# Three orders of work in layer 0's attention of a two-layer decoder trunk

## The chip, the cores and the metric

The kernel runs on one core of one Trainium2 chip. The metric is the device time of one execution in microseconds (us), the median of several runs. A core has engines that each work through their own list of instructions in order: PE (TensorE, matrix products), DVE (VectorE), ACT (ScalarE), POOL (GpSimd) and SP (SyncE, which issues most DMA transfers). An engine waits on semaphores that other engines or DMA queues raise. Matrix products go into PSUM, from which DVE or ACT move them into SBUF.

## The reference

The trunk has two layers on one sequence of 1024 positions with a width of 1024, all in 32-bit floats; the inputs are activations, a memory of 256 rows, positions and the weights. Layer 0 mixes tokens with multi-head latent attention, where queries and keys are expanded from narrow projections and only a part of each head carries rotary positions; layer 1 uses a sliding window. Both add four heads that attend to the memory, and a squared-ReLU MLP follows each.

```python
MLA_HEADS, MLA_Q_RANK, MLA_KV_RANK = 12, 384, 256
MLA_NOPE, MLA_ROPE, MLA_V = 64, 32, 64

def mla_mixer(hn, positions, w_in, q_norm_g, kv_norm_g, w_uq, w_ukv):
    proj = hn @ w_in                       # c_q | c_kv | k_r | q_cross
    ...
    q = (rmsnorm(c_q, q_norm_g) @ w_uq).reshape(b, s, MLA_HEADS, MLA_QK)
    q = jnp.concatenate([q[..., :MLA_NOPE], rope(q[..., MLA_NOPE:], positions)], axis=-1)
    kv = (rmsnorm(c_kv, kv_norm_g) @ w_ukv).reshape(b, s, MLA_HEADS, MLA_NOPE + MLA_V)
    k_nope, v = kv[..., :MLA_NOPE], kv[..., MLA_NOPE:]
    k_rope = jnp.broadcast_to(rope(k_r[:, :, None, :], positions), (b, s, MLA_HEADS, MLA_ROPE))
    k = jnp.concatenate([k_nope, k_rope], axis=-1)
    o = causal_dense_attention(q, k, v)
    return o.reshape(b, s, MLA_HEADS * MLA_V), q_cross

def reference(x, mem, ...):
    mem_n = rmsnorm(mem, mem_norm_g)
    for i in range(DEPTH):                 # DEPTH = 2
        hn = rmsnorm(x, attn_norm_g[i])
        mix, q_cross = mla_mixer(...) if i % 2 == 0 else swa_mixer(...)
        cross = memory_cross_attention(q_cross, mem_n, w_mem_kv[i])
        x = x + jnp.concatenate([mix, cross], axis=-1) @ w_o[i]
        x = x + squared_relu_mlp(rmsnorm(x, mlp_norm_g[i]), mlp_w_up[i], mlp_w_down[i])
    return rmsnorm(x, final_norm_g)
```

## The kernel before, in words

Every large matrix product is made of three: each operand is split into a high part and a low part in a shorter format, and `mm3` or `mm3w` (lines 106 to 121) add high x high, high x low and low x high in PSUM. `split` (line 94) makes the two parts of a tile: ACT copies the high part (line 99, or 102 where a gain scales it), and DVE then subtracts it from the source (line 100, or 103). So whatever is split passes first ACT and then DVE.

The program is built by Python that traces the operations; a scheduler then gives every engine its list. It keeps the traced order unless something moves a block: `tc.issue_after(ins)` puts what is traced inside it behind the instruction `ins` on the engine of `ins`. It adds no wait, and the other engines' lists are ordered without it.

The change lies in the part of layer 0's attention that comes between the narrow projections and the scores (lines 785 to 985; in the profile about 174 to 250 us of 2090). It goes as follows.

*Keys.* A loop over `j`, six blocks of 128 rows of the keys' part without rotation (two heads each): 12 matmuls of 128x512 into `pskn{j}`, one of two PSUM buffers of 128x1024. DVE moves the first half of the columns out into `kn[j]` (shown as `kq`, line 934), ACT the second (line 935).

*Rope weights.* `load_cols` (line 703) is a generator that loads query weights in nine pieces: three blocks of rows `kt` by three thirds of the columns `i`, each a DMA of 192 KB on SP's queue into a staging tile `wraw` (shown as `wr`, with two buffers in turn, line 708), which is then split into high and low parts (`wqrh` on ACT, `wqrl` on DVE). A buffer is free for the next piece once DVE has made the low part. Each step of the generator makes one piece. At `j == 1` the kernel traces all nine pieces of the rotary columns at once.

*Queries.* For each of eight query tiles `t`, `q_rope` makes nine matmuls of 128x384 into `psqr{t}`, three for each block of rows `kt` of the weights, and DVE and POOL apply the rotation (lines 327 to 332). `q_ropeT` transposes the result of tile `t - 2` on PE (`psqt{t}`, line 962), and ACT moves it out (lines 963 and 964). The same loop loads the weights of the part without rotation (`wqn`) through `load_cols`. Then `q_nope(j, i)` makes that part into `psqn{j}_{i}`, moved out by ACT for `i` = 0 and by DVE for `i` = 1 (line 944).

*Head tiles.* `head_tiles(h)` gathers one head's 96 rows of queries and keys by four DMAs on SP's queue into `q32` and `k32` (one buffer each) and splits them. The split tiles of head 0 are `qh, ql, kh, kl`; those of head 1 reuse the memory of `ckh` and `ckl` and are shown by these names.

*Row maxima.* Between the `q_nope` steps, `row_max(0, i)` (line 896) makes the scores of eight row blocks of head 0 once (`psx`), and DVE takes the least negated value of each row into `m_0`. After the last, at `n == 8`, `max_row(0)` (line 884) transposes these values on PE (`psxt`), splits them (`mhl`), and two DMAs put them as a 97th row under the queries of head 0. At `n == 9` follows `head_tiles(1)`. The scores proper (`pss`, line 1038) come next.

`WoHalf` (line 785) loads and splits half of the output weights as a list of eight steps, `todo`; the main loop of the attention takes a step on every third turn from a fixed turn on.

Of the kernel before, what the change touches and what calls it, by code (L numbers as in the profile page):

```python
# [13 lines left out]
AF = mybir.ActivationFunctionType  # L14
# [41 lines left out]
def trunk(  # L56
# [7 lines left out]
    nc = tc.nc  # L64
# [4 lines left out]
    def pool(name, side="left", space=None, bufs=1):  # L69
        kw = {"reuse_waits": "tile"}  # L70
        if space is not None:
            kw["space"] = space
        return tc.alloc_tile_pool(name=name, bufs=bufs, side=side, **kw)
# [5 lines left out]
    def ps2(name):  # L79
        return psum[0].tile([P, 1024], F32, tag="s", bufs=2, name=name)  # L80

    def ps1(name):
        return psum[0].tile([P, 512], F32, tag="m", bufs=4 if len(psum) == 1 else 6, name=name)
# [9 lines left out]
    def f32(ap):  # L93
        return ap.bitcast(F32)

    def split(src, hi, lo, scale=None):

        if scale is None:
            a = nc.scalar.activation(hi, src, AF.Copy)  # L99
            d = nc.vector.tensor_tensor(lo, src, f32(hi), ALU.subtract)  # L100
        else:
            a = nc.scalar.activation(hi, src, AF.Copy, scale=scale)
            d = nc.vector.scalar_tensor_tensor(lo, src, scale, f32(hi), ALU.mult, ALU.subtract)
        return a.ins, d.ins
# [8 lines left out]
    def mm3w(pss, terms):  # L113

        n = len(terms)
        for i, (ah, al, bs) in enumerate(terms):
            for ps, (bh, bl) in zip(pss, bs):
                nc.tensor.matmul(ps, ah, bh, start=i == 0, stop=False)
                nc.tensor.matmul(ps, ah, bl, start=False, stop=False)
            for ps, (bh, bl) in zip(pss, bs):  # L120
                nc.tensor.matmul(ps, al, bh, start=False, stop=i == n - 1)
# [29 lines left out]
    g_q, g_kv, g_mem = gcol[:, 32:35], gcol[:, 35:37], gcol[:, 37:45]  # L151
# [186 lines left out]
    class MemProj:  # L338
# [3 lines left out]
        def __init__(self, layer, pl, src):  # L342
            self.layer, self.pl, self.src = layer, pl, src
# [356 lines left out]
    def wpair(pl, k, n, name, slot):  # L700
        return [pl.tile([P, k, n], F32R, tag=f"{slot}{e}", name=f"{name}{e}") for e in "hl"]

    def load_cols(src, nk, w, outs, g):

        for kt in range(nk):
            for i in range(3):
                raw = wu.tile([P, 4, w], F32, tag="wraw", bufs=2, name=f"wr{w}_{outs[0][1]}_{kt}_{i}")
                nc.sync.dma_start(out=raw.rearrange("p h c -> p (h c)"), in_=src[kt * P : (kt + 1) * P, i * 4 * w : (i + 1) * 4 * w])
                for dst, c0, n in outs:
                    o = [d[:, i * 4 * n : (i + 1) * 4 * n].rearrange("p (h c) -> p h c", c=n) for d in dst[kt]]  # L710
                    split(raw[:, :, c0 : c0 + n], *o, scale=g[:, kt : kt + 1])
                yield

    def rows(w, n):
        return [(w[0][:, k, :], w[1][:, k, :]) for k in range(n)]

    wkn, wkv = rows(wpair(wu, 2, 768, "wkn", "a"), 2), rows(wpair(wu, 2, 768, "wkv", "b"), 2)
    loading = load_cols(mla_w_ukv[0], 2, 128, [(wkv, 64, 64), (wkn, 0, 64)], g_kv)
# [66 lines left out]
    class WoHalf:  # L785


        def __init__(self, layer, half, slot):
            self.layer, self.half, self.slot = layer, half, slot
            self.raw, self.w = {}, []  # L790
            self.todo = [(self.load, 0), (self.load, 1), (self.split, 0), (self.load, 2), (self.split, 1), (self.load, 3), (self.split, 2), (self.split, 3)]

        def step(self):
            if self.todo:
                fn, j = self.todo.pop(0)
                fn(j)
# [61 lines left out]
    def head_ones(i):  # L858
        if i == 0:
            nc.gpsimd.memset(f32(bufs_[0][2][96:97]), 1.0)  # L860
            nc.gpsimd.memset(f32(bufs_[0][3][96:97]), 0.0)
        else:
            for e in (2, 3):
                nc.sync.dma_start(out=f32(bufs_[i][e][96:97]), in_=f32(bufs_[0][e][96:97]))


    def head_tiles(h):
        r = slice((h % 2) * 64, (h % 2) * 64 + 64)
        q32 = hb.tile([96, S], F32, tag="q32", bufs=1, name=f"q32_{h}")
        k32 = hb.tile([96, S], F32, tag="k32", bufs=1, name=f"k32_{h}")  # L870
        nc.sync.dma_start(out=q32[0:64], in_=qn[h // 2][r, :])
        nc.sync.dma_start(out=q32[64:96], in_=qr[h // 4][(h % 4) * 32 : (h % 4) * 32 + 32, :])
        nc.sync.dma_start(out=k32[0:64], in_=kn[h // 2][r, :])
        nc.sync.dma_start(out=k32[64:96], in_=krs)
        qh, ql, kh, kl = bufs_[h % 3]
        if h in (1, 2):
            head_ones(h)
        split(q32, qh[0:96], ql[0:96])
        split(k32, kh[0:96], kl[0:96])
# [3 lines left out]
    def max_row(h):  # L883
        qh, ql, kh, kl = bufs_[h % 3]
        pt = ps1(f"psxt{h}")[0:8, 0:P]
        nc.tensor.transpose(pt, m8s.pop(h), ident)
        if h:
            mh, ml = [at.tile([8, P], F32R, tag=f"m{e}", bufs=2, name=f"m{e}{h}") for e in "hl"]
        else:
            mhl = cp.tile([8, 2, P], F32R, tag="krT", bufs=1, name="mhl0")  # L890
            mh, ml = mhl[:, 0, :], mhl[:, 1, :]
        split(pt, mh, ml)
        nc.sync.dma_start(out=f32(qh[96:97, :]), in_=f32(mh))
        nc.sync.dma_start(out=f32(ql[96:97, :]), in_=f32(ml))

    def row_max(h, i):
        if h not in m8s:
            m8s[h] = hb.tile([P, NT], F32, tag="m8", bufs=2, name=f"m8_{h}")
        qh, ql, kh, kl = bufs_[h % 3]
        n = (i + 1) * P  # L900
        ps = psx(f"psx{h}_{i}") if i > 3 or len(psum) == 1 else ps1(f"psx{h}_{i}")
        cuts = [(0, 320), (320, 640)] if n == 640 else [(a, min(a + 512, n)) for a in range(0, n, 512)]
        if n == 640:
            ps = ps[:, 192:]
        for a, b in cuts:
            nc.tensor.matmul(ps[:, a:b], qh[0:96, i * P : (i + 1) * P], kh[0:96, a:b], start=True, stop=True, skip_group_check=True)  # L906
        m = m8s[h][:, i : i + 1]
        least = 3.0e38
        if h == 0 and i:
            nc.vector.reduce_max(m, ps[:, : n - P], axis=AX, negate=True)  # L910
            least = m
        o, k = (ps[:, n - P : n], dmask) if h == 0 else (ps[:, :n], wide[0][:, S - n :])
        nc.vector.tensor_tensor_reduce(o, o, k, -1.0, least, ALU.add, ALU.min, accum_out=m)  # L913
# [4 lines left out]
    kn = [kq[j // 4][:, j % 4, :] for j in range(6)]  # L918
# [5 lines left out]
    head_ones(0)  # L924
    nc.vector.tensor_copy(krs, krT)
    for j in range(6):
        if j == 1:
            wqr = rows(wpair(wu, 3, 384, "wqr", "b"), 3)
            for _ in load_cols(mla_w_uq[0], 3, 96, [(wqr, 64, 32)], g_q):
                pass  # L930
        ps = ps2(f"pskn{j}")
        mm3w([ps[:, s] for s in halves],
             [(wkn[kt][0][:, j * P : (j + 1) * P], wkn[kt][1][:, j * P : (j + 1) * P], [(ckh[:, kt, s], ckl[:, kt, s]) for s in halves]) for kt in range(2)])
        nc.vector.tensor_copy(kn[j][:, 0:512], ps[:, 0:512])
        nc.scalar.activation(kn[j][:, 512:1024], ps[:, 512:1024], AF.Copy)
    wu2 = pool("wu2", "right")
    wqn = rows(wpair(wu, 2, 768, "wqn", "a"), 2) + rows(wpair(wu2, 1, 768, "wqn2", "c"), 1)
    loading = load_cols(mla_w_uq[0], 3, 96, [(wqn, 0, 64)], g_q)

    def q_nope(j, i):  # L940
        ps = ps1(f"psqn{j}_{i}")
        mm3(ps, [(wqn[kt][0][:, j * P : (j + 1) * P], wqn[kt][1][:, j * P : (j + 1) * P], cTh[:, kt, halves[i]], cTl[:, kt, halves[i]]) for kt in range(3)])
        if i:
            nc.vector.tensor_copy(qn[j][:, halves[i]], ps)
        else:
            nc.scalar.activation(qn[j][:, halves[i]], ps, AF.Copy)
# [30 lines left out]
    for n in range(2, 12):  # L977
        q_nope(n // 2, n % 2)
        for i in range(2 * n - 4, min(2 * n - 2, NT)):
            row_max(0, i)  # L980
        if n == 8:
            max_row(0)
        if n == 9:
            head_tiles(1)
    wu2.release()
    wu.release()
    cp.release()
# [174 lines left out]
    for n in range(len(seq) + LB):  # L1162
# [17 lines left out]
        for g, i in ahead.get(n, ()):  # L1180
            if i < NT:
                row_max(g, i)
            else:
                max_row(g)
        h, j = divmod(n, NB)
# [1043 lines left out]
    for n, (c0, sink, j) in enumerate(jobs):  # L2229
# [17 lines left out]
        for i in range(2):  # L2247
            mid = crossing if n < 3 else swa if n > 5 else None
            ps = feat_mm(w, i, str(n + 2), mid and (lambda: next(mid, None)))
# [75 lines left out]
```

## Time and profile before

| what | value |
|---|---|
| median of 3 runs | 2091.8 us (2091.62 to 2091.94) |
| the profiled execution, own time | 2092.01 us |
| its span, first to last instruction | 2090.3 us |
| mean granted TensorE clock | 1.000 |
| PE busy | 2071.5 us, 99% of the span |
| DVE, ACT, POOL busy | 1474.9, 1109.8, 149.3 us (71%, 53%, 7%) |

The profile shows one execution. A row of a timeline gives the start and the length of an instruction in us, its engine, line, operation and tiles (written, then read after the arrow), how often it stands there in a row, and in brackets the idle time of its engine just before it, with what ended that time. A row of groups gives busy time and mean ns of one, then the idle time before. Matmuls overlap: the length of one is longer than the step from one to the next. SPq is the queue on which SP issues DMAs; the row of a DMA is its issue, not its transfer.

### The profile page before, as it was taken

To read this page: it belongs to the slowest core of one execution; us is meant where nothing else is said; L and a number is where in the kernel's file an instruction comes from. 1 tells how busy PE (TensorE), PEld (TensorE's weight loads), DVE (VectorE), ACT (ScalarE), POOL (GpSimd) and SP (SyncE) were. 2 spreads that over 40 slices of the span, in tenths; PEclk is the share of its full clock that TensorE was granted. 3 is DMA by queue.
4 is the path that set the end of the run, shared out by engine and by line. 5 is a ranking of instruction groups with operands and counts; after the bars stand their busy time and mean duration, and the time that the engine had idled before them with its cause. 6 is when DMAs were issued, how large, how long until landed. Compare 5 with 4: busy or idle time off the path is not lost.

```text
span 2090.3 us, 28907 instructions
## 1 busy us (share of the span) xinstructions
PE 2071.5 (99%) x9744; PEld 1690.3 (81%) x9744; DVE 1474.9 (71%) x2978; ACT 1109.8 (53%) x2396; POOL 149.3 (7%) x265
## 2 busy tenths in 40 slices
PE   9999999999999999999999999999999999999998
PEld 6988777778888888888888888778888888888887
DVE  8766778775977777976558534666977776976565
ACT  7554466666745544444445435766755444444453
POOL 1001001000000000000001133420000000000000
PEclk9999999999999999999999999999999999999999
DMA  6303233342444546944433544542344446944342
GB/s 225 104 1 84 51 70 92 102 146 87 140 153 151 167 152 233 330 132 157 136 116 110 148 100 124 142 132 84 126 153 165 161 142 233 327 145 156 118 120 91
DMA packets 182228, 292.86 MB, mean 140 GB/s; under 512 B 17739, under 2 KB 72128, under 8 KB 182080
## 3 DMA queue, kind: packets, MB, share of 16 engines
q1 hardware_dynamic: 175584, 272.60, 41.5%
q0 software_dynamic: 5168, 15.80, 2.1%
q10 hardware_dynamic: 1328, 2.63, 0.4%
q8 instruction: 76, 1.25, 0.2%
q14 instruction: 72, 0.59, 0.1%
HBM read 187.60 MB, written 81.44 MB: 129 GB/s over the span
## 4 chain that ended last, share of the span: by engine, by line
PE 94%; DVE 3%; ACT 1%; DMA 1%; issue 1%; POOL 0%; SPq 0%; DVEq 0%; ACTq 0%
PE psy L1897 6%; PE psy L1899 6%; PE psy L1898 6%; PE psu L1561 5%; PE psu L1560 5%; PE psu L1559 5%; PE psz L1898 4%; PE psz L1897 4%; PE psz L1899 4%; PE psv L1560 4%; PE psv L1561 4%; PE psv L1559 4%; PE pso L1068 3%; PE pss L1038 3%; PE pswo L109 3%; PE pswo L111 3%
## 5 line engine op out<-in xcount | busy, mean ns | idle before, releaser
L99 ACT ACTIVATE g<-i 128x512 fp32r<-128x512 f32 x79 | 49.9, 631 | 105.8 <-PE psy L1898 51.8
L1897 PE MATMUL psy<-g 128*128 128x512 f32 x256 | 100.0, 390 | 0.0
L1048 ACT ACTIVATE p<-pss 128x512 f32<-128x512 f32 (+2 forms) x144 | 68.8, 487 | 58.5 <-DVE pss L1046 50.1
L1898 PE MATMUL psy<-g 128*128 128x512 f32 x256 | 99.7, 389 | 0.0
L1899 PE MATMUL psy<-g 128*128 128x512 f32 x256 | 99.6, 389 | 0.0
L100 DVE TENSOR_TENSOR g<-i,g 128x512 fp32r<-128x512 f32 x79 | 55.3, 700 | 49.6 <-ACT g L99 49.6
L1068 PE MATMUL pso<-p,vf 128*128 128x512 f32 (+3 forms) x214 | 87.8, 492 | 0.0
L99 ACT ACTIVATE i<-mr 128x512 fp32r<-128x512 f32 x78 | 47.8, 627 | 72.3 <-PE psy L1898 23.6
L99 ACT ACTIVATE uh<-i 128x512 fp32r<-128x512 f32 x66 | 41.6, 631 | 82.9 <-PE psz L1898 38.4
L100 DVE TENSOR_TENSOR uh<-i,uh 128x512 fp32r<-128x512 f32 x66 | 45.6, 690 | 46.5 <-ACT uh L99 46.4
L913 DVE CUSTOM_DVE_ANT_0 psx<-psx,wide 128x1024 f32<-128x1024 f32 (+6 forms) x88 | 66.7, 760 | 14.8 <-PE psx L906 14.5
L1897 PE MATMUL psz<-g 128*128 128x512 f32 x192 | 74.7, 389 | 0.0
L1898 PE MATMUL psz<-g 128*128 128x512 f32 x192 | 74.7, 389 | 0.0
L1899 PE MATMUL psz<-g 128*128 128x512 f32 x192 | 74.7, 389 | 0.0
L1458 ACT ACTIVATE mr<-mr,gcol 128x256 f32<-128x256 f32 (+1 forms) x160 | 63.9, 475 | 13.2 <-DMA mr<-in_mlp_w_up_dram 11.8
L100 DVE TENSOR_TENSOR i<-mr,i 128x512 fp32r<-128x512 f32 x78 | 53.6, 687 | 23.7 <-ACT i L99 23.7
L1779 DVE TENSOR_TENSOR mqq<-mqf,mqq 128x512 f32<-128x512 f32 x64 | 43.1, 686 | 21.7 <-DMA mqf<-in_mlp_w_down_dram 21.6
L1899 PEld LDWEIGHTS psy<-g 128*128 128x128 f32 x256 | 48.1, 188 | 10.0
L1897 PEld LDWEIGHTS psy<-g 128*128 128x128 f32 x256 | 48.1, 188 | 9.8
L1898 PEld LDWEIGHTS psy<-g 128*128 128x128 f32 x256 | 48.1, 188 | 9.8
L1458 ACT ACTIVATE d<-d,gcol 128x256 f32<-128x256 f32 x128 | 53.6, 497 | 0.2 <-DMA d<-in_mlp_w_up_dram 0.2
L2154 ACT ACTIVATE sp<-sp,sst 128x257 f32<-128x257 f32 (+1 forms) x96 | 46.5, 488 | 13.0 <-DVE sst L2152 12.7
(674 smaller groups left out, 6847.9 us busy)
## 6 DMA issues: line engine op xcount, KB each, us to landing
i<-hd SPq DMA_DIRECT2D x154, 256.0 KB
hd<-uh SPq DMA_DIRECT2D x76, 256.0 KB
hd<-ul SPq DMA_DIRECT2D x76, 256.0 KB
mr<-in_mlp_w_up_dram SPq DMA_DIRECT2D x36, 512.0 KB
hd<-x SPq DMA_DIRECT2D x72, 256.0 KB
mr<-hd SPq DMA_DIRECT2D x70, 256.0 KB
d<-in_mlp_w_up_dram SPq DMA_DIRECT2D x32, 512.0 KB
mqf<-in_mlp_w_down_dram SPq DMA_DIRECT2D x32, 512.0 KB
```

What stands on the lines that cost most here:

```text
L99: a = nc.scalar.activation(hi, src, AF.Copy)
L100: d = nc.vector.tensor_tensor(lo, src, f32(hi), ALU.subtract)
L913: nc.vector.tensor_tensor_reduce(o, o, k, -1.0, least, ALU.add, ALU.min, accum_out=m)
L1048: masked[1:] = [nc.scalar.activation(p[:, c0:], ps, AF.Exp, scale=SC).ins]
L1068: mms.append(lambda: nc.tensor.matmul(o, a, b, skip_group_check=True, **kw))
L1458: nc.scalar.activation(w[:, k, :], w[:, k, :], AF.Copy, scale=g_mlp[layer][:, k0 + k : k0 + k + 1])
L1559: nc.tensor.matmul(ps, wh[:, k, :], xh[:, k, :], start=p in (1, 2, 5) and k == 0, stop=False, skip_group_check=True)
L1560: nc.tensor.matmul(ps, wh[:, k, :], xl[:, k, :], start=False, stop=False, skip_group_check=True)
L1561: nc.tensor.matmul(ps, wl[:, k, :], xh[:, k, :], start=False, stop=k == 3, skip_group_check=True)
L1897: nc.tensor.matmul(ps, ah[:, j, :], bh, start=start, stop=False, skip_group_check=True)
L1898: nc.tensor.matmul(ps, ah[:, j, :], bl, start=False, stop=False, skip_group_check=True)
L1899: nc.tensor.matmul(ps, al[:, j, :], bh, start=False, stop=k == NP - 1, skip_group_check=True)
```

## The change

There are three edits, and a step that does nothing.

1. The rope weights' pieces are no longer traced all together at `j == 1`. The generator is made at `j == 0`, and three pieces are traced after each of the first three blocks of keys, with their ACT parts behind that block's move on ACT.
2. `max_row` returns the two instructions of its split, and `head_tiles(1)` is traced behind both of them, on ACT and on DVE.
3. The list of steps of the output weights' half 0 of layer 0 gets a step without work before its last.

```diff
--- before.py
+++ after.py
@@ -789,6 +789,8 @@
             self.layer, self.half, self.slot = layer, half, slot
             self.raw, self.w = {}, []
             self.todo = [(self.load, 0), (self.load, 1), (self.split, 0), (self.load, 2), (self.split, 1), (self.load, 3), (self.split, 2), (self.split, 3)]
+            if layer == half == 0:
+                self.todo.insert(-1, (lambda j: None, 0))
 
         def step(self):
             if self.todo:
@@ -889,9 +891,10 @@
         else:
             mhl = cp.tile([8, 2, P], F32R, tag="krT", bufs=1, name="mhl0")
             mh, ml = mhl[:, 0, :], mhl[:, 1, :]
-        split(pt, mh, ml)
+        done = split(pt, mh, ml)
         nc.sync.dma_start(out=f32(qh[96:97, :]), in_=f32(mh))
         nc.sync.dma_start(out=f32(ql[96:97, :]), in_=f32(ml))
+        return done
 
     def row_max(h, i):
         if h not in m8s:
@@ -924,15 +927,16 @@
     head_ones(0)
     nc.vector.tensor_copy(krs, krT)
     for j in range(6):
-        if j == 1:
+        if j == 0:
             wqr = rows(wpair(wu, 3, 384, "wqr", "b"), 3)
-            for _ in load_cols(mla_w_uq[0], 3, 96, [(wqr, 64, 32)], g_q):
-                pass
+            loading = load_cols(mla_w_uq[0], 3, 96, [(wqr, 64, 32)], g_q)
         ps = ps2(f"pskn{j}")
         mm3w([ps[:, s] for s in halves],
              [(wkn[kt][0][:, j * P : (j + 1) * P], wkn[kt][1][:, j * P : (j + 1) * P], [(ckh[:, kt, s], ckl[:, kt, s]) for s in halves]) for kt in range(2)])
         nc.vector.tensor_copy(kn[j][:, 0:512], ps[:, 0:512])
-        nc.scalar.activation(kn[j][:, 512:1024], ps[:, 512:1024], AF.Copy)
+        with tc.issue_after(nc.scalar.activation(kn[j][:, 512:1024], ps[:, 512:1024], AF.Copy).ins):
+            for _ in range(3):
+                next(loading, None)
     wu2 = pool("wu2", "right")
     wqn = rows(wpair(wu, 2, 768, "wqn", "a"), 2) + rows(wpair(wu2, 1, 768, "wqn2", "c"), 1)
     loading = load_cols(mla_w_uq[0], 3, 96, [(wqn, 0, 64)], g_q)
@@ -979,9 +983,10 @@
         for i in range(2 * n - 4, min(2 * n - 2, NT)):
             row_max(0, i)
         if n == 8:
-            max_row(0)
+            done = max_row(0)
         if n == 9:
-            head_tiles(1)
+            with tc.issue_after(done[0]), tc.issue_after(done[1]):
+                head_tiles(1)
     wu2.release()
     wu.release()
     cp.release()
```

ScalarE (ACT) from the first block of keys on, before. `kq<-pskn` is a block's move out of PSUM, `wqrh<-wr_64_kt_i` the high part of the rope weights' piece (kt, i), and `kh<-k_0` the split of head 0's keys:

```order
L102 ACTIVATE wqrh<-wr_64_0_2_1981,gcol 128x128
L102 ACTIVATE wqrh<-wr_64_1_0_1985,gcol 128x128
L935 ACTIVATE kq_1942<-pskn_1956 128x512
L102 ACTIVATE wqrh<-wr_64_1_1_1989,gcol 128x128
L935 ACTIVATE kq_1942<-pskn_2009 128x512
L102 ACTIVATE wqrh<-wr_64_1_2_1993,gcol 128x128
L99 ACTIVATE kh_1951<-k_0_2342 96x1024
L102 ACTIVATE wqrh<-wr_64_2_0_1997,gcol 128x128
L935 ACTIVATE kq_1942<-pskn_2024 128x512
```

And now, from the move of block 0:

```order
L937 ACTIVATE kq_1942<-pskn_1958 128x512
L102 ACTIVATE wqrh<-wr_64_0_0_1973,gcol 128x128
L102 ACTIVATE wqrh<-wr_64_0_1_1977,gcol 128x128
L937 ACTIVATE kq_1942<-pskn_1985 128x512
L99 ACTIVATE kh_1951<-k_0_2342 96x1024
L102 ACTIVATE wqrh<-wr_64_0_2_1981,gcol 128x128
L102 ACTIVATE wqrh<-wr_64_1_0_2000,gcol 128x128
L937 ACTIVATE kq_1942<-pskn_2012 128x512
L102 ACTIVATE wqrh<-wr_64_1_1_2004,gcol 128x128
```

Four pieces stood ahead of block 0's move, and none does now; block 2's move, which had seven ahead of it, has four.

TensorE (PE) at the first rope matmuls of the queries, before (`psqr_2091`, `psqr_2117` and `psqr_2143` are query tiles 0, 1 and 2):

```order
L109 MATMUL psqr_2091<-wqrh,cTh 128x384
L110 MATMUL psqr_2091<-wqrl,cTh 128x384
L111 MATMUL psqr_2091<-wqrh,cTl 128x384
L109 MATMUL psqr_2117<-wqrh,cTh 128x384
L110 MATMUL psqr_2117<-wqrl,cTh 128x384
L111 MATMUL psqr_2117<-wqrh,cTl 128x384
```

And now, from the 18th of these matmuls to the first transpose (`psqt_2165` is that of tile 0):

```order
L111 MATMUL psqr_2143<-wqrh,cTl 128x384
L109 MATMUL psqr_2091<-wqrh,cTh 128x384
L109 MATMUL psqr_2117<-wqrh,cTh 128x384
L109 MATMUL psqr_2143<-wqrh,cTh 128x384
L110 MATMUL psqr_2091<-wqrl,cTh 128x384
L111 MATMUL psqr_2091<-wqrh,cTl 128x384
L110 MATMUL psqr_2117<-wqrl,cTh 128x384
L111 MATMUL psqr_2117<-wqrh,cTl 128x384
L110 MATMUL psqr_2143<-wqrl,cTh 128x384
L111 MATMUL psqr_2143<-wqrh,cTl 128x384
L966 MATMUL psqt_2165<-ident,fa_101 128x128 x3
```

Each tile's nine matmuls stood together; now tiles 0, 1 and 2 go through the first two row blocks of the weights first (18 matmuls), and then all three through the last.

VectorE (DVE) at the last row maximum of head 0 (`m_0`, `psx_7`), the split of the transposed maxima (`mhl`) and the splits of head 1 (`ckh`, `ckl`), before:

```order
L944 COPY qn_1941<-psqn_1_2442 128x512
L910 TENSOR_REDUCE m_0_2362<-psx_7_2426 128x1
L100 TENSOR_TENSOR ckh<-q_1_2482,ckh 96x1024
L913 ISA psx_7_2426,m_0_2362<-psx_7_2426,dmask,m_0_2362 128x128
L913 ISA m_0_2362 128x1
L100 TENSOR_TENSOR mhl_2466<-psxt_2464,mhl_2466 8x128
L944 COPY fa_101<-psqn_1_2471 128x512
```

And now:

```order
L913 TENSOR_REDUCE m_0_2362<-psx_7_2426 128x1
L916 ISA psx_7_2426,m_0_2362<-psx_7_2426,dmask,m_0_2362 128x128
L916 ISA m_0_2362 128x1
L100 TENSOR_TENSOR mhl_2466<-psxt_2464,mhl_2466 8x128
L100 TENSOR_TENSOR ckh<-q_1_2482,ckh 96x1024
L948 COPY fa_101<-psqn_1_2471 128x512
L100 TENSOR_TENSOR ckl<-k_1_2483,ckl 96x1024
```

The split of head 1's queries stood between the two steps of the last row block; it stands behind the split of the maxima now.

TensorE (PE) at the first score tile (`pss_1_0`), with the semaphores that it waits for, before and then now:

```order
L1038 MATMUL pss_1_0_2557<-qh_1949,kh_1951 128x512 [waits DMAHW0_49,Activation_49]
```

```order
L1043 MATMUL pss_1_0_2557<-qh_1949,kh_1951 128x512 [waits DMAHW5_49,DVE_49]
```

The matmul stands at the same place in the row, but its PSUM buffer is another: the engine that must have emptied it was ACT and is DVE.

## The prediction

> **What bounds the kernel now.** I read the page first: busy shares and the chain of waits.
>
> ```profile
> PE 2071.5 (99%) x9744; PEld 1690.3 (81%) x9744; DVE 1474.9 (71%) x2978; ACT 1109.8 (53%) x2396; POOL 149.3 (7%) x265
> PE 94%; DVE 3%; ACT 1%; DMA 1%; issue 1%; POOL 0%; SPq 0%; DVEq 0%; ACTq 0%
> ```
>
> TensorE sets the end. It has no slack in which a delay could vanish, and no engine after this stage gets another order, so a microsecond by which TensorE stands still longer or shorter here moves the end by a microsecond. The question is therefore only where PE waits between about 175 and 250 us, now and afterwards. The stretches by stage and the list of PE's waits answer the first half:
>
> ```profile
> 180.00:186.00 6.00, 5.24 (x24) 4.00 (x23) 2.63 (x5) 3.13 (x6) 0.00 (x0) 1.00 0.55 142
> 192.00:198.00 6.00, 6.00 (x38) 5.96 (x37) 6.00 (x17) 2.81 (x6) 2.80 (x5) 1.00 0.63 166
> 220.00:230.00 10.00, 8.97 (x41) 6.85 (x41) 8.16 (x21) 2.41 (x4) 0.00 (x0) 1.00 0.08 24
> PE psxt L886 <- DVE m L913: 1.0, 1, 1.0
> PE pskn L118 <- ACT kq L935: 0.8, 1, 0.8
> ```
>
> The first numbers are the stretch, its length and PE's busy time; 1.00 near the end is the granted clock. PE loses 0.8 us at the fifth block of keys and 1.0 us at the transpose of the row maxima. Nothing else in the stage makes it wait. These two are all that the change can win, about 2 us of 2091.8, or 0.1%. A measurement of this kernel tells about 0.2% (4.2 us) from no change.
>
> **The change part by part.** *Stall at the fifth block of keys.* A block is 12 matmuls into one of two PSUM buffers; block 4 (counted from 0) waits for ScalarE's move of block 2.
>
> ```profile
> 184.59 0.61 PE L121 MATMUL pskn<-ckh,wknl 128*128 128x512 f32 x2
> 185.96 0.50 PE L118 MATMUL pskn<-ckh,wknh 128*128 128x512 f32 x1 [0.76 <-ACT kq L935]
> 173.35 0.68 ACT L102 ACTIVATE wqrh<-wr,gcol 128x128 fp32r<-128x128 f32 x2
> 177.85 0.60 ACT L935 ACTIVATE kq<-pskn 128x512 f32<-128x512 f32 x1 [0.38 <-DVE kq L934]
> 183.07 0.40 ACT L102 ACTIVATE wqrh<-wr,gcol 128x128 fp32r<-128x128 f32 x1 [1.68 <-DMA wr<-in_mla_w_uq_dram]
> 184.07 1.06 ACT L99 ACTIVATE kh<-k 96x1024 fp32r<-96x1024 f32 x1 [0.60 <-DMA k<-kq]
> 185.33 0.58 ACT L935 ACTIVATE kq<-pskn 128x512 f32<-128x512 f32 x1
> 179.32 0.52 SPq L873 DMA_DIRECT2D k<-kq  x1
> ```
>
> The pair from 184.59 would let block 4 start at 184.59 + 2 x 0.23 = 185.05; it starts at 185.96, so 0.91 us are lost. Block 2's move stood ready behind the weight piece at 183.07 and the split kh, which waited for its DMA.
>
> Now ScalarE has kh, two weight pieces, then block 2's move. The DMA behind kh is issued once block 0 has been moved (177.85 + 0.60, so 178.5 instead of 179.32). In the old run it took 184.07 - 179.32 = 4.75 us; a DMA of the same 64 x 1024 without company took 3.08:
>
> ```profile
> 212.14 0.58 SPq L871 DMA_DIRECT2D q<-qn  x1
> 215.22 1.06 ACT L99 ACTIVATE qh<-q 96x1024 fp32r<-96x1024 f32 x1 [1.40 <-DMA q<-qn]
> ```
>
> So kh starts between 181.6 and 183.25, block 2's move 1.0 + 0.6 later, and it ends at 183.8 to 185.4. That returns 0.91 to 0.5 us. But block 3's move then sits behind piece (1,1), whose load starts only when VectorE has split piece (0,2), 1.8 us after kh's start: 1.8 + 2.3 (load, below) + 0.4 + 0.6 = 5.1 us after kh's start, 186.7 to 188.35, against a demand at 187.8 to 188.3. At the late end the stall is moved one block on. I take -0.3 (bounds -0.9 and, with one slow load, +0.9), nearer the late end, since 4.75 is that very DMA's row and two loads still follow it closely.
>
> *The last weight piece.* The queries' rope matmuls need nine pieces in two staging buffers: the load of the ninth, (2,2), can start only when VectorE has split the seventh. That split now stands behind VectorE's move of the last block; before it stood ahead.
>
> ```profile
> 191.10 0.62 PE L121 MATMUL pskn<-ckh,wknl 128*128 128x512 f32 x2
> 191.55 0.33 PE L109 MATMUL psqr<-wqrh,cTh 128*128 128x384 f32 x1
> 191.75 0.69 DVE L934 COPY kq<-pskn 128x512 f32<-128x512 f32 x1 [0.72 <-PE pskn L121]
> 192.36 0.48 DVE L103 SCALAR_TENSOR_TENSOR wqnl<-wr,gcol,wqnh 128x256 fp32r<-128x256 f32 x1
> L103 DVE SCALAR_TENSOR_TENSOR wqrl<-wr,gcol,wqrh 128x128 fp32r<-128x128 f32 x9 | 3.0, 349 | 3.8 <-ACT wqrh L102 3.6
> 174.16 0.33 SPq L708 DMA_DIRECT2D wr<-in_mla_w_uq_dram  x1
> 176.45 0.40 ACT L102 ACTIVATE wqrh<-wr,gcol 128x128 fp32r<-128x128 f32 x1 [1.90 <-DMA wr<-in_mla_w_uq_dram]
> 178.88 0.33 SPq L708 DMA_DIRECT2D wr<-in_mla_w_uq_dram  x1
> 190.25 0.39 ACT L102 ACTIVATE wqrh<-wr,gcol 128x128 fp32r<-128x128 f32 x1
> 196.09 0.34 PE L111 MATMUL psqr<-wqrh,cTl 128*128 128x384 f32 x1
> 196.26 0.49 PE L962 MATMUL psqt<-ident,fa 128*128 128x128 f32 x3
> ```
>
> Let E be the moment when PE leaves the keys (191.55 before; ScalarE's part of the last piece was done at 190.64, ahead of it). Now: the move starts at E + 0.20 and takes VectorE 0.61 until its next instruction, the seventh split 0.35, the load from issue to use 176.45 - 174.16 = 2.29, ScalarE's split 0.40: E + 3.85, and some 0.1 of handing over. PE's new order does 18 matmuls first, at (196.26 - 191.55)/27 = 0.174 each: 3.14. So PE waits +0.8. The other load above took 183.07 - 178.88 = 4.19; with such a one the wait is 2.7. I take +0.9, as the short row had no other large transfer beside it and here little runs beside it either.
>
> The Trainium skill, DMA: Bandwidth & Descriptors, section Anatomy of one DMA, fits 2.0 us + bytes/436e3 (for the other kind of queue); for 192 KB that is an estimate of 2.45 us, and the wait by it 0.95 with no long tail. The 4.19 of this trace does not agree with it.
>
> *The first transposed query tile.* PE is in order, and behind 27 matmuls stands the transpose of tile 0, which needs VectorE's and GpSimd's rotation. Its last matmul was the ninth; now it is the 23rd.
>
> ```profile
> 193.94 0.35 DVE L327 TENSOR_TENSOR fa<-psqr,trig 128x192 f32<-128x192 f32 x1
> 195.31 0.78 POOL L332 TENSOR_TENSOR fa<-fa,rb 128x192 f32<-128x192 f32 x1
> ```
>
> The rotation took from 193.94 to 196.09, 2.15 us, and ended 0.17 before PE came. Let K be the moment at which the last piece lets PE go on. Tile 0's last matmul starts at K + 4 x 0.174 and lasts 0.34; 0.1 later VectorE starts; the rotation ends at K + 3.3. PE comes at K + 9 x 0.174 = K + 1.57. That is 1.7; GpSimd's two steps can be 0.2 to 0.4 shorter where nothing runs beside them, so +1.6 (1.3 to 1.9).
>
> *The tiles behind it.* The load chain of the next weights (wqn) starts 3 us later too and its splits lie between the rotations on VectorE; and transpose 1 now gets the PSUM buffer of transpose 0, so it waits for ScalarE's moves. VectorE needs 4 x 0.27 + 0.48 = 1.6 us a tile, PE's pace is 1.9 (nine matmuls and three transposes), so VectorE catches up. I take +0.4, from 0 to 1.0.
>
> *The row maxima.* VectorE did a split of head 1 between the last reduction and the last minimum:
>
> ```profile
> 227.28 1.21 DVE L100 TENSOR_TENSOR ckh<-q,ckh 96x1024 fp32r<-96x1024 f32 x1
> 228.41 0.35 DVE L913 CUSTOM_DVE_ANT_0 psx<-psx,dmask,m 128x128 f32<-128x128 f32 x1
> 227.45 0.39 PE L111 MATMUL psqn<-cTh,wqn2l 128*128 128x512 f32 x1
> 228.87 0.27 PE L886 MATMUL psxt<-ident,m 128*8 128x128 f32 x1 [1.03 <-DVE m L913]
> ```
>
> Behind it in the new order, the minimum comes 228.41 - 227.28 = 1.13 earlier; PE was free from 227.45 + 0.23 = 227.68 and lost 1.19. I take -1.1 (-1.2 to -0.9). Head 1's splits now start after 229.5, and their first reader is a matmul about 237, some 8 us later; that hides them. The next loads of head 2 on SP wait for those splits, and are read after 243.
>
> *The first scores.* The first score tile has been given another PSUM buffer: it had that of the last but one query tile, emptied by ScalarE one tile earlier; it now has that of the very last, which VectorE empties.
>
> ```profile
> 235.15 0.40 PE L1038 MATMUL pss<-qh,kh 97*128 97x512 f32 x1
> 235.42 0.69 DVE L944 COPY fa<-psqn 128x512 f32<-128x512 f32 x1 [3.46 <-PE psqn L111]
> ```
>
> PE started at 235.15 while that move ran from 235.42 to 236.11; now it must wait for its end: +1.0 (0.9 to 1.2).
>
> *The empty step in the output weights' list* moves no row on any engine: 0.
>
> **Sum**: -0.3 + 0.9 + 1.6 + 0.4 - 1.1 + 1.0 = +2.5 us. The profiled execution took 2092.0 (span 2090.3 and 1.7 around it), 0.2 above the median of the timed runs; so 2094.5 against it, and 2094.3 as a median of runs. All low ends together give -0.9 + 0.8 + 1.3 + 0 - 1.2 + 0.9 = +0.9; all high ends +0.9 + 2.7 + 1.9 + 1.0 - 0.9 + 1.2 = +6.8.
>
> **The rivals.** *A slow load on the chain (slower).* If one load on which PE waits takes 4.19 instead of 2.29, as the row at 178.88 did, the sum is 2.5 + 1.9 = +4.4: 2096.2. It decides from a load time of about 4.0 on. For it: the late rope weights turn every load from (1,1) on into a link of one chain, and one row of two above was that slow. Against: it needs to fall on the piece that PE waits for.
>
> *The new waits are hidden (a little faster).* If the rope weights come in time after all, the two old stalls go (-0.9 - 1.1) and only the buffer's +1.0 stays: 2090.8. For it: in the old run the last piece came 0.9 before PE needed it. Against: the seventh split stands behind the last move by order, so the 3.9 us cannot shrink.
>
> *The clock.* Two or three waits within 5 us could cost PE its clock: at half of it 4 us of matmuls would take 8, +4 on top, 2098.3. Against: the granted clock stayed at 1.00 in the stretch 220:230, with 1.03 us idle in it. The Trainium skill, TensorE: Matmul & The Clock Gate, section A second HAM failure mode, describes such a loss from short pauses at PSUM buffers; this trace, at 1.00 beside its stalls, does not show it.
>
> *The change doesn't do what it says*: true of the empty step only.
>
> **How the numbers follow.** Forecast, +0.9 to +4.2: 0.62. Slow load, above +4.2: 0.25. Clock: 0.03. Hidden waits, between -4.2 and +0.9: 0.07. Faster by over 4.2 has no mechanism, since the stalls that can go are 2 us; 0.03 for what I don't see. So slower by over 0.2% 0.28, within 0.2% 0.62 + 0.07 = 0.69, faster 0.03. The range runs from 0, halfway between the lowest sum and the hidden waits, to +5.6, which takes in most of the slow load: 2091.8 to 2097.4. Left out are the clock, the faster case, most of the hidden waits and the slow load's upper end, together somewhat under 0.2.
>
> **What would show it.** In the new profile: block 4's wait gone or cut, at most a small one at block 5; a wait of about 0.9 us of psqr for wqrh; about 1.6 us of psqt for GpSimd or VectorE; psxt's wait gone; about 1 us of pss for VectorE's move of the last query tile. If psqr and psqt do not wait, the load chain is misread; if PE shows these waits and the time stays, TensorE is not what sets the end.

## The result, and the profile after

The changed kernel takes 2095.02 us (median of 22 runs, 2093.83 to 2096.63), the kernel before 2091.42 beside it (22 runs, 2090.65 to 2092.69). The ratio is 1.0017, with a 95% interval of 1.0011 to 1.0023: slower by 2.3 to 4.8 us, 3.6 by the medians, where 2.5 were forecast. The profiled execution took 2094.62 with a span of 2092.9, 2.6 more than the span before.

The busy share says nothing, again: the engines' row of the page, and the shares of the chain that ended last.

```profile
PE 2072.5 (99%) x9744; PEld 1690.3 (81%) x9744; DVE 1476.0 (71%) x2978; ACT 1109.2 (53%) x2396; POOL 148.1 (7%) x265
PE 91%; DVE 3%; ACT 3%; DMA 2%; issue 1%; POOL 0%; DVEq 0%; ACTq 0%
```

PE's waits between 174 and 260 us (engine, line, what it waited for: us in total, times, longest) show what has changed. The two waits of before, at `pskn` and `psxt`, are gone, and three others stand in their place; that of `psx` is in before too:

```profile
PE psqt L966 <- POOL fa L332: 1.6, 2, 1.3
PE pss L1043 <- DVE fa L948: 0.9, 1, 0.9
PE psqr L109 <- ACT wqrh L102: 0.7, 1, 0.7
PE psx L909 <- ACT p L1053: 0.6, 1, 0.6
```

The same by stretches (length, PE busy, ...; the granted clock is third from the end). PE is fuller from 180 to 186 and from 220 to 230 than before, and loses 2.4 us between 192 and 206 (2.05 and 0.32); the clock stays at 1.00 through these pauses:

```profile
180.00:186.00 6.00, 5.87 (x27) 4.53 (x26) 2.65 (x6) 2.72 (x5) 0.00 (x0) 1.00 0.34 99
192.00:198.00 6.00, 3.95 (x22) 3.31 (x20) 2.92 (x10) 1.17 (x3) 1.25 (x3) 1.00 0.44 128
198.00:206.00 8.00, 7.68 (x48) 7.25 (x49) 6.69 (x21) 4.42 (x13) 5.20 (x9) 1.00 0.35 95
220.00:230.00 10.00, 10.00 (x46) 7.80 (x45) 8.33 (x25) 0.77 (x2) 0.00 (x0) 1.00 0.16 39
```

To turn this into a sum, the same instructions of PE are set side by side. First the start of the keys, and the second transposed tile, in the trace of before (the other starts of before are in the prediction), then the marks of the changed kernel:

```profile
163.53 0.47 PE L118 MATMUL pskn<-ckh,wknh 128*128 128x512 f32 x1
198.16 0.38 PE L962 MATMUL psqt<-ident,fa 128*128 128x128 f32 x2
```

```profile
163.16 0.47 PE L118 MATMUL pskn<-ckh,wknh 128*128 128x512 f32 x1
184.96 0.50 PE L118 MATMUL pskn<-ckh,wknh 128*128 128x512 f32 x1
190.73 0.33 PE L109 MATMUL psqr<-wqrh,cTh 128*128 128x384 f32 x1
194.77 0.79 PE L109 MATMUL psqr<-wqrh,cTh 128*128 128x384 f32 x3 [0.73 <-ACT wqrh L102]
197.95 0.55 PE L966 MATMUL psqt<-ident,fa 128*128 128x128 f32 x3 [1.32 <-POOL fa L332]
200.39 0.55 PE L966 MATMUL psqt<-ident,fa 128*128 128x128 f32 x3 [0.32 <-POOL fa L332]
230.13 0.27 PE L888 MATMUL psxt<-ident,m 128*8 128x128 f32 x1
237.41 0.50 PE L1043 MATMUL pss<-qh,kh 97*128 97x512 f32 x1 [0.85 <-DVE fa L948]
```

| mark | after minus before, us | step |
|---|---|---|
| first block of keys | 163.16 - 163.53 = -0.37 | |
| fifth block of keys | 184.96 - 185.96 = -1.00 | -0.63 |
| first rope matmul | 190.73 - 191.55 = -0.82 | +0.18 |
| first transposed tile | 197.95 - 196.26 = +1.69 | +2.51 |
| second | 200.39 - 198.16 = +2.23 | +0.54 |
| row maxima | 230.13 - 228.87 = +1.26 | -0.97 |
| first scores | 237.41 - 235.15 = +2.26 | +1.00 |

From the first mark to the last that is 2.26 + 0.37 = 2.63 us. Behind it, from the first scores to the start of PE's last matmul, the two traces have the same length (1848.62 before, 1848.58 after).

### The profile page after: what moved, and what is told of

The parts are those of the page before. It is cut to its first block, busy times and chain, and to the rows that moved or that the text cites. A ratio compares the mean times of both kernels' runs of the same rounds, so it can differ in the third digit from the quotient of the medians.

```text
span 2092.9 us, 28902 instructions
## 1 busy us (share of the span) xinstructions
PE 2072.5 (99%) x9744; PEld 1690.3 (81%) x9744; DVE 1476.0 (71%) x2978; ACT 1109.2 (53%) x2396; POOL 148.1 (7%) x265
## 3 DMA queue, kind: packets, MB, share of 16 engines
q10 hardware_dynamic: 1328, 2.63, 0.3%
## 4 chain that ended last, share of the span: by engine, by line
PE 91%; DVE 3%; ACT 3%; DMA 2%; issue 1%; POOL 0%; DVEq 0%; ACTq 0%
PE psy L1903 6%; PE psy L1904 6%; PE psy L1902 6%; PE psu L1564 5%; PE psu L1566 5%; PE psu L1565 5%; PE psz L1903 4%; PE psz L1904 4%; PE psz L1902 4%; PE psv L1566 4%; PE psv L1564 4%; PE psv L1565 4%; PE pso L1073 3%; PE pss L1043 3%; PE pswo L109 3%; PE pswo L111 3%
```

## The experiments

The times in one table. The stage is the time from the start of the first `pskn` matmul to that of the first `pss` matmul, the rest that from there to the start of PE's last matmul, each from one trace (worked out before rounding, so they can differ by 0.01 from the rows). The kernels were timed in groups, each with the kernel before beside it; the ratio is taken over the runs and is not quite the quotient of the two medians (for e1 that would be 0.9996).

| kernel | median us | before beside it | ratio (95%) | stage | rest |
|---|---|---|---|---|---|
| before | 2091.42 | | | 71.63 | 1848.62 |
| after | 2095.02 | 2091.42 | 1.0017 (1.0011 to 1.0023) | 74.25 | 1848.58 |
| e1 head order alone | 2090.93 | 2091.79 | 0.9999 (0.9990 to 1.0008) | 70.26 | 1848.78 |
| e2 rope weights alone | 2095.93 | 2091.79 | 1.0021 (1.0012 to 1.0030) | 74.07 | 1848.57 |
| e3 tile by tile | 2095.70 | 2091.79 | 1.0019 (1.0011 to 1.0028) | 74.47 | 1848.85 |
| e4 not held | 2090.44 | 2091.79 | 0.9994 (0.9985 to 1.0003) | 69.98 | 1848.38 |
| e5 one block later | 2097.89 | 2091.47 | 1.0027 (1.0017 to 1.0037) | 74.64 | 1850.62 |
| e6 rotary columns only | 2090.62 | 2091.47 | 0.9995 (0.9986 to 1.0004) | 70.01 | 1848.94 |
| e7 last move on ACT | 2094.39 | 2091.47 | 1.0013 (1.0004 to 1.0022) | 73.05 | 1848.99 |
| e8 as e6, not held | 2091.23 | 2091.47 | 0.9997 (0.9988 to 1.0006) | 69.81 | 1849.82 |
| e9 before again | 2091.69 | 2092.31 | 0.9998 (0.9989 to 1.0007) | 72.05 | 1848.46 |
| e10 after again | 2094.86 | 2092.31 | 1.0014 (1.0005 to 1.0023) | 73.89 | 1850.00 |
| e11 as e4, again | 2090.50 | 2092.31 | 0.9992 (0.9983 to 1.0002) | 70.81 | 1848.63 |

### Each edit alone

e1 has only the second edit, e2 only the first:

```diff
-        split(pt, mh, ml)
+        done = split(pt, mh, ml)
...
+        return done
...
-            max_row(0)
+            done = max_row(0)
         if n == 9:
-            head_tiles(1)
+            with tc.issue_after(done[0]), tc.issue_after(done[1]):
+                head_tiles(1)
```

> Only the second edit: head 1's tiles behind the split of the row maxima, the rope weights as before. My theory (each step of time is a wait of PE in this stage with a cause of its own): the transpose psxt no longer waits for the last minimum, PE gains 1.0 to 1.2 us, the first scores keep a buffer emptied by ACT and don't wait, the fifth block's 0.8 us wait stays: 1.1 us below before, ratio 0.9995. Rival (head 1's splits, now later, become late for their first reader): a new wait of PE of 0.5 us or more between 230 and 250 us, time equal to before.

```diff
-        if j == 1:
+        if j == 0:
...
-            for _ in load_cols(mla_w_uq[0], 3, 96, [(wqr, 64, 32)], g_q):
-                pass
+            loading = load_cols(mla_w_uq[0], 3, 96, [(wqr, 64, 32)], g_q)
...
-        nc.scalar.activation(kn[j][:, 512:1024], ps[:, 512:1024], AF.Copy)
+        with tc.issue_after(nc.scalar.activation(kn[j][:, 512:1024], ps[:, 512:1024], AF.Copy).ins):
+            for _ in range(3):
+                next(loading, None)
```

> Only the first edit: rope weights three pieces per block, each behind the block's move on ACT, head 1's tiles as before. My theory: the sum of the rope terms in the trace of the changed kernel, -0.6 at the fifth block, +0.9 at psqr, +1.6 and +0.5 at psqt, and +1.0 at the first scores, whose buffer is DVE's here too: 3.4 to 3.6 us above before, ratio 1.0017. Rival (the two edits act on each other, for instance the buffer's wait comes from head 1's order): no wait at the first scores, 2.4 us above before.

PE's waits from 174 to 250 us in e1, then from 170 to 262 in e2:

```profile
PE psx L907 <- ACT p L1050: 0.6, 1, 0.6
PE pskn L118 <- ACT kq L936: 0.4, 1, 0.4
```

```profile
PE psqt L963 <- POOL fa L332: 1.3, 1, 1.3
PE psxt L886 <- DVE m L913: 1.0, 1, 1.0
PE pss L1039 <- DVE fa L945: 0.9, 1, 0.9
PE psx L906 <- ACT p L1049: 0.6, 1, 0.6
PE psqr L109 <- ACT wqrh L102: 0.6, 1, 0.6
```

In e1 the wait at `psxt` is gone, no wait takes its place, and the stage is 70.26, 1.37 shorter than before; 0.3 of that is the fifth block, which waits 0.4 in place of 0.8, though nothing in e1 bears on it. By the medians e1 is 0.9 below before, which its interval does not tell from no change. In e2 the wait at `psxt` is as before, and the three new waits are all there, that at the first scores too: they belong to the rope weights alone. The buffer of the first scores is thus an effect of the first edit and not of the two together, as the rival had it. e2's stage is 2.4 longer than before, less than the 3.4 to 3.6 expected: here the fifth block did not wait at all and one of the two waits at `psqt` did not occur. By the medians it is 4.1 longer.

### Does PE's new order cost, or the late piece?

```diff
     for t in range(NT):
-        q_rope(t)
+        if t in (1, 2):
+            with tc.issue_after(last_mm):
+                q_rope(t)
+        else:
+            q_rope(t)
```

(`last_mm` is the last matmul of the tile before.)

> The changed kernel, with PE's rope matmuls forced back to nine in a row for each query tile. My theory (the late last piece of the rope weights sets it, and PE's new order only places the wait): the wait moves to tile 0's last row block, 2.6 to 3.0 us at psqr in place of 0.7, no wait at psqt; the first scores have a buffer emptied by ACT here, so their 0.9 us go too: 0.5 to 1.0 us below the changed kernel, 2.6 to 3.1 above before. Rival (PE's new order, with the transpose close behind its matmuls, is what costs): psqr waits 0.7 as now, psqt not at all, and the time is 2.6 below the changed kernel, 1 above before.

PE's waits in e3 from 170 to 262 us:

```profile
PE psqr L109 <- ACT wqrh L102: 2.7, 1, 2.7
PE psqt L969 <- POOL fa L333: 0.6, 1, 0.6
PE psx L910 <- ACT p L1060: 0.6, 1, 0.6
PE psqr L109 <- ACT qr L971: 0.4, 1, 0.4
```

With tile 0 first, PE waits 2.7 us for the same piece, and the stage has not become shorter though the first scores no longer wait. The rival is out: it asked for 0.7 at `psqr` and a time 1 above before. My number of 2.6 to 3.0 held for this wait; that no others would remain did not, as a transpose and a buffer still cost 0.6 and 0.4. The 18 matmuls that the scheduler put first fill most of the wait for the last piece; taking them away gains nothing: e3 is 3.9 above before by the medians, where 2.6 to 3.1 were expected. The buffer of the first scores follows PE's order: they wait in all five traces in which the first 18 matmuls run ahead (after, e2, e5, e7, e10) and in none of the eight in which each tile's nine stand together.

### Where the pieces stand

e4 traces the pieces in threes from block 0 on, but does not hold them behind the moves. e5 holds them, but behind the moves of blocks 1 to 3.

```diff
-        with tc.issue_after(nc.scalar.activation(kn[j][:, 512:1024], ps[:, 512:1024], AF.Copy).ins):
-            for _ in range(3):
-                next(loading, None)
+        nc.scalar.activation(kn[j][:, 512:1024], ps[:, 512:1024], AF.Copy)
+        for _ in range(3):
+            next(loading, None)
```

> The changed kernel, with the pieces traced three per block from block 0 on but not held behind the block's move on ACT. My theory (it is the place behind the moves that makes the last piece late): the scheduler puts the pieces ahead of the moves about as before, psqr and psqt don't wait, the fifth block's wait is between 0.3 and 0.9 us, psxt doesn't wait: about 1.1 us below before, ratio 0.9995, like the kernel with the second edit alone. Rival (tracing them in threes from the first block on is what costs): 1 us or more above before, with waits at psqr or psqt.

```diff
-        if j == 0:
+        if j == 1:
...
-            for _ in range(3):
+            for _ in range(3 if j else 0):
                 next(loading, None)
```

> The changed kernel, with the pieces behind the moves of blocks 1, 2 and 3 in place of 0, 1 and 2. PE's order is that of the changed kernel; on DVE the seventh split still stands directly behind the last block's move. My theory (a chain of loads, each waiting for the split two before it, sets when the ninth piece is there): the chain starts one block (2.8 us) later, and takes the slack that it has ahead of the last move; the last piece comes 1.0 to 1.5 us later, psqr waits 1.7 to 2.2 us in place of 0.7, 1 to 1.5 above the changed kernel, ratio to before 1.0023. Rival (the seventh split's place behind the last move alone sets it): psqr waits 0.7 as before, same time as the changed kernel.

In e4 PE waits nowhere from 174 to 250 us but at `psx` as ever. The trace of e5 has, from 174 to 262 us:

```profile
PE psqr L109 <- ACT wqrh L102: 1.9, 1, 1.9
PE psqt L966 <- DVE fa L329: 1.7, 1, 1.7
PE pss L1043 <- DVE fa L948: 0.9, 1, 0.9
PE psx L909 <- ACT p L1053: 0.6, 1, 0.6
```

So it is the hold behind the moves that costs, not the tracing in threes. And it is a chain. With a start one block (2.7 us) later PE waits 1.2 us longer for the last piece (1.9 against 0.7), as expected, though the seventh split stands behind the last move in both. DVE's row of that split in e5:

```profile
192.09 0.35 DVE L103 SCALAR_TENSOR_TENSOR wqrl<-wr,gcol,wqrh 128x128 fp32r<-128x128 f32 x1 [1.13 <-ACT wqrh L102]
```

It starts 2.03 us after PE leaves the keys at 190.06, and had to wait for its piece; in the changed kernel it starts 0.81 after. Counted from the start of the keys, the last piece's split on ACT comes 0.6 and 1.1 us later than in the two traces of the changed kernel; the rest of the longer wait is that PE leaves the keys earlier. e5's stage is only 0.4 to 0.8 above the two traces of the changed kernel, since no second transpose waits, and its median is 2.9 above; more on that below.

### The chain broken

e6 loads only the rotary columns, in three DMAs; the nine splits stay behind the first three moves. e8 does the same without the hold.

```diff
+    def load_rope():
...
+        src = mla_w_uq[0].rearrange("n (h c) -> n h c", c=96)
+        for kt in range(3):
+            raw = wu.tile([P, 12, 32], F32, tag="wraw", bufs=2, name=f"wrr_{kt}")
+            nc.sync.dma_start(out=raw, in_=src[kt * P : (kt + 1) * P, :, 64:96])
+            for i in range(3):
+                o = [d[:, i * 128 : (i + 1) * 128].rearrange("p (h c) -> p h c", c=32) for d in wqr[kt]]
+                split(raw[:, 4 * i : 4 * i + 4, :], *o, scale=g_q[:, kt : kt + 1])
+                yield
...
-            loading = load_cols(mla_w_uq[0], 3, 96, [(wqr, 64, 32)], g_q)
+            loading = load_rope()
```

> The changed kernel, with the rope weights loaded in three DMAs of only the 32 rotary columns of each head (128 rows by 12 heads, 128 bytes in one stretch), one for each block of rows, into the same two buffers; the nine splits stay, three behind each of the first three blocks' moves. My theory (the late last piece comes from nine loads through two buffers): only the third load has to wait for a buffer, the last piece is there before the last block of keys, psqr and psqt don't wait, nor does the fifth block nor psxt nor the first scores (buffer emptied by ACT): 2.0 us below before, ratio 0.9990. Rival (the place of the splits behind the moves is what costs): waits of 0.5 us or more at psqr, psqt or pskn, time equal to before or above it.

> As the run before the last but one, three loads of the rotary columns alone, but without holding the splits behind the moves: the scheduler puts the first three ahead of block 0's move. My theory: the same 2.0 us below before, as the last piece has time either way; a wait of up to 0.4 us at a block of keys where a split stands ahead of a move. Rival (splits ahead of the moves cost the fifth block's wait): the fifth block waits 0.5 us or more, 1.3 us below before.

e6's PE waits from 174 to 250 us:

```profile
PE psx L909 <- ACT p L1064: 0.6, 1, 0.6
PE psqr L109 <- ACT qr L979: 0.2, 1, 0.2
```

The splits stand behind the moves as in the changed kernel, and the waits for the last piece, for the rotation and at the first scores are gone; PE goes tile by tile again. So the hold costs only together with the nine loads through two buffers. (e6 also moves only a third of the bytes; the runs do not part that from the number of loads.) The stage is 1.6 shorter than before (expected 2.0; a buffer costs 0.2). e8's stage is the shortest of all, and no block of keys waits. By the medians neither can be told from before: they are 0.9 and 0.2 us below it, where 2.0 was expected of both.

### The first scores' buffer

```diff
-        if i:
+        if i and j < 5:
             nc.vector.tensor_copy(qn[j][:, halves[i]], ps)
```

> The changed kernel, with the last query tile's second half moved out of PSUM by ACT and not by DVE. My theory (the first scores wait for the very last query tile's move, whoever makes it): the wait stays at 0.7 to 0.9 us, now for ACT, and the time is that of the changed kernel within 0.2. Rival (DVE is the cause, being late with the move): the wait goes, 0.9 us below the changed kernel.

```profile
PE pss L1043 <- ACT fa L950: 0.7, 1, 0.7
```

The wait is there with ACT as well, about 0.1 shorter than with DVE (0.75 in PE's row, 0.85 in the two traces of the changed kernel). It is not DVE that is late: the very last query tile has to be moved out before PE may write there, whichever engine moves it. The median is 2.9 above before, 0.7 less than that of the changed kernel, where at most 0.2 was expected; in e7's trace the fifth block and the second transpose do not wait, which the edit does not explain.

### Three kernels again

> The kernel before once more, unchanged, timed against itself. What is open: the medians of the changed kernel and before are 3.6 us apart, the stage in the two traces only 2.6. My theory (the trace of before caught a slow start: its waits at 44 and 49 us are 0.3 to 0.9 us longer than in every other trace, outside the changed part): this trace has the shorter waits at the start, a span about 0.6 below the first one, the 0.8 us wait at the fifth block and the 1.0 at psxt again; ratio 1.0000 with an interval of 0.001 to either side. Rival (the waits at the start belong to the kernel before, and the change removes them): the same long waits at 44 and 49 us.

> The changed kernel once more, unchanged. My theory: the same waits within 0.3 us each (psqr 0.7, psqt 1.6, pss 0.9, none at pskn and psxt), 3 to 3.6 us above before. Rival (the loads on the chain differ from one execution to the next, and the first trace caught a short one): psqr waits over 1.2 us here, or the stage is more than 3.2 us longer than in before.

> Once more the version of the fourth run: the pieces traced three per block from block 0 on and not held, head 1's tiles behind the row maxima. My theory: none of the five waits in the stage, the stage 1.8 to 2.0 us shorter than in before and 4.4 to 4.6 shorter than in the changed kernel, 1.3 to 1.9 us below before. Rival (the first trace was lucky with the fifth block): a wait of 0.3 to 0.8 us at the fifth block, 1.1 below before.

The kernel before against itself gave 0.9998 (0.9989 to 1.0007), so a comparison of 11 runs can be 0.6 us off. My idea of the slow start held by half: this trace of before starts its keys 0.26 us earlier (163.27 against 163.53), but lost 1.2 and not 0.8 at the fifth block, so the span is the same 2090.3. The changed kernel's waits came again, with 0.7 at `psqr`, 1.7 at `psqt` and 0.9 at `pss`: the chain was not caught at a lucky moment, and its stage of 73.89 is 1.84 above this one of before. e11 shows that e4's fifth block had been lucky; PE's row of e11, and ACT's row ahead of it, then the same row of ACT in e4:

```profile
185.85 0.50 PE L118 MATMUL pskn<-ckh,wknh 128*128 128x512 f32 x1 [0.74 <-ACT kq L937]
184.26 1.06 ACT L99 ACTIVATE kh<-k 96x1024 fp32r<-96x1024 f32 x1 [0.35 <-DMA k<-kq]
```

```profile
183.35 1.06 ACT L99 ACTIVATE kh<-k 96x1024 fp32r<-96x1024 f32 x1 [0.54 <-DMA k<-kq]
```

The split `kh` stands ahead of block 2's move on ACT and waits for its DMA; that came 0.9 us later (0.7 counted from the start of the keys), and the block waited 0.74. e4 is the version with the lowest times, 1.35 and 1.81 us below before in two comparisons. It beats the changed kernel clearly; against before, both intervals still just hold 1.

## Why the prediction was right, step by step

**What bounds the kernel.** PE's waits in this stage moved the end: 2.63 us in the stage, 2.6 in the span.

**The fifth block (-0.3, bounds -0.9 to +0.9)** gave -0.63, and 0.18 of it came back by the last block: -0.45. The last matmuls of block 3 and the move of block 2 in the changed kernel:

```profile
184.22 0.61 PE L121 MATMUL pskn<-ckh,wknl 128*128 128x512 f32 x2
184.33 0.57 ACT L937 ACTIVATE kq<-pskn 128x512 f32<-128x512 f32 x1
```

The move's end at 184.90 lies in the forecast 183.8 to 185.4. PE could have gone on at 184.22 + 2 x 0.23 = 184.68 and started at 184.96, so 0.28 are still lost, too little for the list of waits. In the second trace of the changed kernel nothing is lost here. The size hangs on the DMA behind `kh`, as e4 and e11 show.

**The last piece (+0.9).** The rows of the steps, on DVE, SP's queue and ACT:

```profile
190.93 0.69 DVE L936 COPY kq<-pskn 128x512 f32<-128x512 f32 x1 [1.85 <-PE pskn L121]
191.54 0.60 DVE L103 SCALAR_TENSOR_TENSOR wqrl<-wr,gcol,wqrh 128x128 fp32r<-128x128 f32 x2
191.91 0.34 SPq L708 DMA_DIRECT2D wr<-in_mla_w_uq_dram  x1
194.32 0.40 ACT L102 ACTIVATE wqrh<-wr,gcol 128x128 fp32r<-128x128 f32 x1 [2.06 <-DMA wr<-in_mla_w_uq_dram]
```

With E = 190.73, the move starts at E + 0.20, the split at E + 0.81, the load takes 194.32 - 191.91 = 2.41 (forecast 2.29), and PE goes on at E + 4.04 where 3.95 were forecast. The 18 matmuls end at E + 3.13, so 0.91 are lost. The slow load of 4.19 did not come on this link in either trace of the changed kernel. The fit in the Trainium skill, DMA: Bandwidth & Descriptors, section Anatomy of one DMA, is for the other kind of queue; worked out for this load it is an estimate of 2.45 us. The measured 2.41 agrees with it.

**The first transposed tile (+1.6).** The rotation's first row on DVE and its last on POOL:

```profile
195.96 0.36 DVE L327 TENSOR_TENSOR fa<-psqr,trig 128x192 f32<-128x192 f32 x1
197.30 0.59 POOL L332 TENSOR_TENSOR fa<-fa,rb 128x192 f32<-128x192 f32 x1
```

From K = 194.77 it starts at K + 1.19 and ends at K + 3.12 (forecast 3.3); PE's last matmul ahead of it starts at 196.29, so it came at 196.46 and waited 1.49. The table's +2.51 is 0.91 + 1.49 and 0.1 of handing over. **The tiles behind it (+0.4)** cost 0.54. PE's row at 200.39 puts 0.32 of it down to GpSimd's rotation of tile 1, in the second trace 0.43, and not to ScalarE's moves, so VectorE did not catch up as fast as the prediction had it; in e2 the second transpose does not wait. **The row maxima (-1.1)** gave -0.97, and e1 shows that nothing else is needed for it. **The first scores (+1.0)** cost 1.00, and e7 that any engine's move would.

The sum was 2.5 and the traces give 2.63 and 1.84. The slow load and the hidden waits did not happen. What the steps don't give is the rest of the medians' 3.6. The interval from 2.3 to 4.8 holds the stage's 2.6, and the second comparison gave 2.55, but both medians of the changed kernel stand above what their stages say, by 1.0 and 0.7 us, and those of e2, e3 and e5 by 1.1 to 3.4.

The **clock** rival is not shown to be the reason. A drop of the granted clock, at another place than I had put it, is in the second trace of the changed kernel and in e5's (below). The mean granted clock of each timed run is on record with three digits, and such a drop is 0.0008 of it, so it is a hint only: 0.998 or less stands beside 3 of 33 runs of the changed kernel and 3 of 89 of before, but beside 7 of 11 of e3 and 5 of 9 of e5. Runs of the changed kernel and of before with the same 0.999 still differ by 3.2 us (medians 2094.96 of 25 runs and 2091.76 of 65). In e5 the clock is thus seen to be part of the rest, and in e3 it may be; for the changed kernel the cause of some 0.7 to 1.0 us stays open.

**The empty step (0).** From 236 us on, every engine's instructions stand in the same order of operations and tiles in the traces of before and of the changed kernel, and the two have the same length there. The step moved nothing.

## What to carry to other kernels

Where loads go through two buffers in turn, the order of the splits is a chain: put its first link behind something late, and the last load comes later too, though by less (here 2.7 us at the first link made 0.6 to 1.1 at the last). A reordering is costed by following each wait to the instruction that PE reaches next; the price here was waits at three places, and only one of them was at the moved work. A buffer handed out by turns is part of an order too: moving one instruction can give a later one the buffer that is freed last.

## What the runs showed of the hardware

The column "rest" is 1848.4 to 1849.0 in ten of 13 traces and 1849.8 to 1850.6 in e5, e8 and e10. All three lose it at the same place, some 200 us behind the change, where PE turns to the output projection. The stretch from 436 to 444 us in e10, and then that from 434 to 444 us in e9, the kernel before (PE busy next, the clock third from the end):

```profile
436.00:438.00 2.00, 1.48 (x6) 0.59 (x4) 1.91 (x4) 1.64 (x6) 0.00 (x0) 1.00 0.92 244
438.00:440.00 2.00, 1.65 (x7) 0.91 (x7) 1.94 (x5) 1.89 (x6) 0.00 (x0) 1.00 1.01 386
440.00:442.00 2.00, 2.00 (x5) 1.44 (x6) 1.94 (x4) 0.63 (x1) 0.00 (x0) 0.55 0.95 364
442.00:444.00 2.00, 2.00 (x7) 1.59 (x6) 1.94 (x7) 1.54 (x3) 0.00 (x0) 0.60 0.09 36
```

```profile
434.00:436.00 2.00, 1.30 (x5) 0.42 (x4) 1.91 (x4) 1.63 (x7) 0.00 (x0) 1.00 0.86 272
436.00:438.00 2.00, 1.83 (x7) 1.09 (x8) 1.94 (x5) 1.70 (x5) 0.00 (x0) 1.00 1.05 402
438.00:440.00 2.00, 2.00 (x9) 1.40 (x9) 1.91 (x5) 0.63 (x1) 0.00 (x0) 1.00 0.84 322
440.00:442.00 2.00, 2.00 (x11) 1.63 (x10) 1.97 (x7) 1.73 (x3) 0.00 (x0) 1.00 0.01 5
442.00:444.00 2.00, 2.00 (x11) 1.65 (x10) 1.91 (x5) 1.85 (x4) 0.00 (x0) 1.00 0.00 0
```

In e10 the granted clock falls to 0.50 behind pauses of 0.52 and 0.35 us in two stretches, and stays there from 440.2 to 443.6, some 3.4 us as in e5 and e8; by the two rows that is a loss of up to 0.45 x 2 + 0.40 x 2 = 1.7 us. The matmuls go through at half the rate (5 and 7 in two stretches, 11 and 11 in e9). The pauses alone do not bring it about: e9 has 0.70 and 0.17 us of them at the same place of the program, the same sum, and keeps 1.00, as do nine other traces. The Trainium skill, TensorE: Matmul & The Clock Gate, section A second HAM failure mode: psum-queue depth-cycling, describes a clock that goes back and forth between half and full speed when PE pauses often between groups of matmuls. These rows agree with it in the two speeds; they show one drop, not a going back and forth. In the changed stage, with 0.9, 1.5 and 0.5 us of pauses within 7 us, the clock stayed at 1.00. e8 is among the three and is not a slowed kernel, and one trace of the changed kernel has the drop while the other does not, so the drop is no effect of the change that these traces show; whether the changed kernel meets it more often stays open.
